# Ordering the large stages of a two-layer encoder trunk from a job list, with 110 seven-product pairs

## The chip, the cores and the metric

The kernel runs on one core of a Trainium2 chip. The time is device microseconds for one execution; the median of three runs of the kernel before is 2484.49 us (2484.1 to 2484.86). Five engines matter: TensorE (PE, matmuls, with its weight loads listed as PEld), VectorE (DVE), ScalarE (ACT), GpSimd (POOL) and the queue of SyncE (SP) that issues nearly all transfers. Each engine works through its own instructions in program order and waits for others by semaphores.

## The reference: what is computed

Two layers on a sequence of 256 tokens with 2048 channels, all in float32. Layer 0 mixes tokens with a gated MLP (gMLP), layer 1 with latent attention (MLA, 16 heads); each is followed by a gated MLP with a causal convolution of width 3 over time.

```python
def gmlp_mixer(x, w_in, ln_g, ln_b, w_s, b_s, w_out):
    z = jax.nn.gelu(x @ w_in)                     # 2048 -> 2 x 6144
    u, v = jnp.split(z, 2, axis=-1)
    v = layer_norm(v, ln_g, ln_b)                 # then mixed over windows of 128 tokens with masked w_s
    ...
    return (u * s.reshape(B, S, GM_HALF)) @ w_out # 6144 -> 2048

def conv_ffn(x, w_up, conv_w, conv_b, w_down):
    h = x @ w_up                                  # 2048 -> 2 x 5504
    h = lax.conv_general_dilated(h, conv_w[:, None, :], ...) + conv_b   # three taps per channel, causal
    a, g = jnp.split(h, 2, axis=-1)
    return (jax.nn.silu(g) * a) @ w_down          # 5504 -> 2048

# each sub-layer: x <- layer_norm(ALPHA * x + sublayer(x)); layer 0: gMLP, FFN; layer 1: MLA, FFN
```

## The kernel before

**Matrix products.** Every float32 operand is split into two float32r parts, a high one (ACT's cast, `hi`, `wh` in the profile) and the remainder (a DVE subtraction, `lo`, `wl`). A product of two operands is three matmuls: high x high, high x low, low x high. Weights come from HBM as one 1 MB tile per *step* (two pieces of 512 KB, 128 x 2048 values, `raw`), and a plain step takes two blocks of 128 input channels (`k`) times 1024 output channels for both halves of the 256 tokens: 8 block products of 128 x 512 columns, 24 matmuls.

**Seven-product pairs.** A step marked `seven` computes the same 2 x 2 x 2 block product in the manner of Strassen and Winograd with seven products, 21 matmuls. For this, sums of the weight blocks are made (DVE, in place in `raw`), split again (`th` by ACT, `tl` by DVE), and sums of the activations too (`xs` once per sub-layer, or `sums1` for each pair of a down product). Its products go to four extra PSUM banks (`up_p`, `dn_p`, ...), which are combined by `gather` at the end of the group. Before, 89 steps are marked.

**Stages in order.** v: 6 groups of 8 steps; u: 6 groups, after each of which the gating (transposes `uT`, products `s`, `gates`); wo: 48 steps in two halves (`Down`); boundary; up: 10 groups of 8 steps, each followed by 16 transposes (`ht`) and the convolution (`taps`); two tail steps; dn: 44 steps in two halves; boundary; MLA; boundary; up and dn again; the last norm. A `boundary` finishes the last steps of a down product (three of them, `LATE`, held back), normalises, transposes the new activations and begins the next product; its order is written out by hand.

**Memory.** One pool of 22 slots of 1 MB each (`BIG`) holds weight tiles in all their forms, the activations (four slots), their sums, and results; a plain step needs 2 slots when it is split, a seven-product step 4, and a tile that is loaded and not yet split 1. Small pools hold intermediate tiles (`mid`, 3 tiles; `t2`, 5), and PSUM has 8 banks.

**What sets the order.** Inside the large stages program order is the order in which Python emits the instructions (`Pinned`, line 74 in all rows of the profile). One step of PE work is one tick: `Feed.next` splits up to two steps ahead and loads up to two more, as far as `room` allows, and `Flow` holds small tasks at ticks counted from the present one (`flow.at(2, "mid", ...)`): the parts of `taps`, of `gather`, `out`, `gates`, `split4`, `sums1`. These distances are fixed numbers in the code. `Ordered` does the same for weight loads on the SP queue; residuals, the norm's rows and the gate's tables are issued with `nc.sync` and have no such place.

**Convolution.** For four tiles of 128 channels x 256 tokens, `taps` writes the three scaled copies with ACT out of PSUM (12 operations), adds them shifted with DVE (two operations of 4 x 255 and 4 x 254 values), then `silu` (ACT) and the gate (DVE).

**Attention scores.** Per head and per half of the queries five matmuls of 256 columns go to one PSUM bank; for the first 128 queries only the first 128 keys are read afterwards.

Of the kernel before, what the change touches and what calls it, by code (L numbers as in the profile page):

```python
# [8 lines left out]
F32 = mybir.dt.float32  # L9
# [96 lines left out]
class Feed:  # L106
# [20 lines left out]
    def _close(self):  # L127
        if self.open is not None:
            s, raw = self.open
            for c in self._pairs(s):  # L130
                self.ve.tensor_tensor(c(s.tl), c(raw), c(s.th.bitcast(F32)), ALU.subtract)
            self.open = None

    def _pairs(self, s):

        if s.by_k:
            return [lambda t: t[:, 1024:2048], lambda t: t[:, 0:1024]]
        four = lambda t: t.rearrange("p (a b c) -> p a b c", a=2, b=2)
        return [lambda t: four(t)[:, :, 1], lambda t: four(t)[:, :, 0]]

    def _split(self, between=lambda: None):
# [4 lines left out]
        s.hi, s.lo = self._tile("wh", F32R), self._tile("wl", F32R)  # L146
# [7 lines left out]
        if s.seven:  # L154
            s.th, s.tl = self._tile("th", F32R), self._tile("tl", F32R)
            b21, x, y, b12 = (raw[:, i * 512 : (i + 1) * 512] for i in range(4))
            b22, b11 = (x, y) if s.by_k else (y, x)
            first, second = self._pairs(s)
# [5 lines left out]
            ac.copy(second(s.th), second(raw))  # L164
            self.open = (s, raw)
        self.split += 1

# [16 lines left out]
    def sums(self, s):  # L184

        t2, t1 = (512, 1024) if s.by_k else (1024, 512)
        return [(s.th[:, o : o + 512], s.tl[:, o : o + 512]) for o in (t1, t2, 1536, 0)]
# [40 lines left out]

def placed(pairs, sevens):
# [15 lines left out]
def trunk(ctx: ExitStack, tc: tile.TileContext, x, xT, gm_in, gm_wout, ffn_up, ffn_dn,  # L245
# [40 lines left out]
    def back(src, n_k, sevens):  # L286
        r = []
        for half in range(2):
            o = half * 1024
            for k in back_order(n_k, half):  # L290
                n = min(2, n_k - k)
                r.append(Step([(j * 1024, 1024, src[k + j][:, o : o + 1024]) for j in range(n)], n * 1024,
                              tuple(range(k, k + n)), True, k in sevens[half]))
        return r
# [25 lines left out]
    feed = Feed(sq, ve, ac, big, steps)  # L320
    Pinned.on = Ordered.on = True
# [75 lines left out]
    def split4(src8, q, n, name):  # L397
# [3 lines left out]
        src = src8[:, 2 * (q % 2) : 2 * (q % 2) + 2]  # L401

        def each(f):
            for w, k in ((2, 2),) if n == 4 else ((n // 2, 2), (n // 2 + 1, 1)):
# [3 lines left out]
        each(lambda x, hi, lo: ac.copy(hi, x))  # L408
        flow.at(1, "mid", lambda: each(lambda x, hi, lo: ve.tensor_tensor(lo, x, hi.bitcast(F32), ALU.subtract)))
        return t  # L410
# [27 lines left out]
    def sums1(kk, name):  # L438

        k0, k1 = kk[:, 0, :], kk[:, 1, :]  # L440
        t = tp.tile([P, 4, P], F32, tag="t2", name=f"{name}t", bufs=T2)
        r = tp.tile([P, 2, 512], F32R, tag="mid", name=name, bufs=MID)
        blocks(k0, k1, [t[:, i, :] for i in range(4)])
        flat = t.rearrange("p i t -> p (i t)")
        flow.at(1, "mid", lambda: ac.copy(r[:, 0], flat))
        flow.at(2, "mid", lambda: ve.tensor_tensor(r[:, 1], flat, r[:, 0].bitcast(F32), ALU.subtract))
        return r
# [7 lines left out]
    class Square:  # L455
# [49 lines left out]
        def gather(self, name):  # L505

            e = slot([P, 4, 512], name)
            u2 = tp.tile([P, 512], F32, tag="t2", name=f"{self.tag}u2", bufs=T2)
            p1, p5, p6, p7 = self.p
            ac.copy(e[:, 0], p1)  # L510
            ve.tensor_tensor(u2, e[:, 0], p6, ALU.add)
            ve.tensor_tensor(e[:, 2], u2, p7, ALU.add)
            ve.tensor_tensor(e[:, 1], u2, p5, ALU.add)
            ve.tensor_tensor(e[:, 3], e[:, 2], p5, ALU.add)
            self.e, self.p = e, None

        def out(self, name, func=None):

            z = self.z = slot([P, 4, 512], name) if self.e is None else self.e

            def add():
                for f in range(2):
# [3 lines left out]
            def copy():  # L526
                for f in range(2):
                    for b in range(2):
# [4 lines left out]
                        elif self.e is None:  # L533
                            ac.copy(o, src)

            if self.e is not None:
                flow.at(0, "first", add)
            flow.at(0, "mid", copy)
            return z
# [17 lines left out]
    def square(tag, order, xs, sums, name, room):  # L557

        sq = Square(tag)
        sevens = [i for i, (_, sv) in enumerate(order) if sv]  # L560
        for i in range(len(order)):
            s = tick(room(i))
            sq.step(s, xs, sums, i == len(order) - 1)
            if sevens and i == sevens[-1]:
                flow.at(1, "first", lambda: sq.gather(name))
            tock()
        return sq

    class Down:

        def __init__(self, n_k, src8, sevens, tag):
            self.n_k, self.src8, self.sevens, self.tag = n_k, src8, sevens, tag
            self.hl, self.sums = {}, {}

        def need(self, k, half):
            q = k // 4
            if q not in self.hl:
                self.hl[q] = split4(self.src8[k // 8], q, min(4, self.n_k - 4 * q), f"{self.tag}a{half}_{q}")

        def need_sums(self, k, half):  # L580
            if k in self.sevens[half] and k not in self.sums:
                self.sums[k] = sums1(self.src8[k // 8][:, k % 8 // 2], f"{self.tag}s{half}_{k}")

        def begin(self):
            flow.at(0, "mid", lambda: self.need(0, 0))
            flow.at(1, "mid", lambda: self.need(4, 0))

        def run(self, ln):
            hl, sums = self.hl, self.sums
            for half in range(2):  # L590
# [4 lines left out]
                late = []  # L595
                for i, k in enumerate(order):
                    for j in order[i : i + 4]:
                        flow.at(0, "mid", lambda j=j: self.need(j, half))
                    for j in order[i : i + 5]:
                        flow.at(0, "mid", lambda j=j: self.need_sums(j, half))  # L600
                    left = n - 1 - i
                    if half == 0:
                        s = tick(BIG - 9 - (2 if left < 7 else 0))
                        if left == 6:
                            ln.residual()
                    else:
                        room = BIG - 5 - (k + 7) // 8 - (2 if left < 6 else 0)
                        s = tick(room, splits=2, loads=2 if left > 1 else 1)
                        if left == 5:
                            ln.prep()  # L610
                    if half == 1 and left < LATE:
                        late.append((s, {k // 4: hl[k // 4]}, left == 0))
                        tock()
                        continue
                    sq.step(s, hl, sums, left == 0)
                    rest = order[i + 1 :]
                    if half == 1 or left >= KEEP:
                        if not any(j // 4 == k // 4 for j in rest):
                            del hl[k // 4]
                    if k in sevens:  # L620
                        del sums[k]
                        if not any(j in sevens for j in rest):
                            flow.at(1, "first", lambda sq=sq, half=half: sq.gather(f"{self.tag}e{half}"))
                            flow.at(2, "mid", lambda sq=sq, half=half: ln.add(2 * half, sq))
                    tock()
                if half == 0:
                    for b in range(2):
                        for f in range(2):
                            flow.at(0, "first", lambda b=b, f=f, sq=sq: ln.join(b, f, sq.acc[b][f]))
                            flow.at(1, "mid", lambda b=b, f=f: ln.stat(b, f))  # L630
            flow.flush()
# [70 lines left out]
    class Norm:  # L702
# [21 lines left out]
        def prep(self):  # L724
            i = self.idx
            self.g = slot([P, D], f"lng{i}")
            nc.sync.dma_start(self.g, ln_rows[2 * i : 2 * i + 1, :].to_broadcast([P, D]))
            self.b = slot([P, D], f"lnb{i}")
            nc.sync.dma_start(self.b, ln_rows[2 * i + 1 : 2 * i + 2, :].to_broadcast([P, D]))
# [74 lines left out]
    def tables():  # L804
        nc.sync.dma_start(wTg, w_sT)
        nc.gpsimd.memset(wTg[64:P, :, 0:64], 0.0)
        nc.sync.dma_start(bsb.rearrange("p g i -> p (g i)"), b_s.to_broadcast([P, 1024]))

    def rows():
# [8 lines left out]
        flow.at(1, "mid", copy)  # L818

    for i, q in enumerate(quads):  # L820
        flow.at(2 + i, "mid", lambda q=q: sums.update(sums_quad(xraw[q], q, f"xs0_{q}")))
    flow.at(4, "mid", tables)
    flow.at(6, "post", rows)

# [3 lines left out]

    for gi in range(6):
        base = BIG - 4 - len(quads) - gi  # L830
# [671 lines left out]
```

## Time and profile before

| what | value |
|---|---|
| median of three runs | 2484.49 us |
| the profiled execution's own time | 2485.57 us |
| its span, first to last instruction | 2483.8 us |
| mean granted TensorE clock | 0.998 |
| PE busy | 2470.1 us (99%) |
| PE weight loads busy | 2068.6 us (83%) |
| DVE busy | 2049.6 us (83%) |
| ACT busy | 1444.2 us (58%) |
| HBM read and written | 482.29 MB and 8.39 MB, 198 GB/s over the span |

Busy time counts each engine's time with at least one instruction in flight. Matmuls overlap in their pipeline, so the duration shown for one is longer than the distance from one start to the next; the distance is what adds up. A group of instructions is written as output<-inputs by tile names with buffer numbers left out, then its shapes and count, the busy time in us and the mean of one in ns, and the idle time of the engine right before, with what ended it. The chain of waits follows the work that ended last backwards; its pieces show start, length, engine and output tile, with a count.

### The profile page before, as it was taken

Reading aid. Unit: us, or ns where it says so; the run is one execution under the profiler, and the core shown is the slowest. Engines: PE = TensorE matmul, PEld = TensorE weight load, DVE = VectorE, ACT = ScalarE, POOL = GpSimd, SP = SyncE. Lnnn points to the kernel's source line nnn. Section 1 sums busy time; section 2 is a strip of 40 time slices with the busy share of each in tenths; the row PEclk is TensorE's granted clock in tenths of the full one; section 3 lists DMA queues with packets and bytes.
Section 4 is the critical chain, followed back from the end, with each engine's and each line's share of the span. In section 5 each row is a group of like instructions: output and inputs, shape, how many; then the busy total and the mean of one; then the engine's idle time right before and its main releaser. Section 6 shows DMA issues by size and latency. Waiting matters only on the chain.

```text
span 2483.8 us, 30045 instructions
## 1 busy us (share of the span) xinstructions
PE 2470.1 (99%) x11666; PEld 2068.6 (83%) x11666; DVE 2049.6 (83%) x2121; ACT 1444.2 (58%) x1673; POOL 1.9 (0%) x11
## 2 busy tenths in 40 slices
PE   9999999999999999999999999999999999999998
PEld 7888888888888888888888888988888888888886
DVE  7899888889797678888899887757768888889796
ACT  6455645555454566666665454555466666667552
POOL 0000000000000000000000000000000000000000
PEclk9999999999999999999999999999999999999999
DMA  7555645555666645555456665435555555556664
GB/s 308 191 193 197 206 167 170 202 171 203 220 214 235 229 166 174 204 186 203 153 198 237 226 237 210 173 136 213 203 174 207 171 187 202 189 196 202 226 205 151
DMA packets 119662, 492.64 MB, mean 198 GB/s; under 512 B 13280, under 2 KB 13664, under 8 KB 104928
## 3 DMA queue, kind: packets, MB, share of 16 engines
q1 hardware_dynamic: 118512, 484.31, 55.6%
q10 hardware_dynamic: 1008, 6.42, 0.6%
q8 instruction: 91, 1.49, 0.2%
q14 instruction: 51, 0.42, 0.0%
HBM read 482.29 MB, written 8.39 MB: 198 GB/s over the span
## 4 chain that ended last, share of the span: by engine, by line
PE 98%; DVE 1%; DMA 0%; ACT 0%; issue 0%; DVEq 0%; ACTq 0%
PE up L74 30%; PE dn L74 16%; PE u L74 9%; PE wo L74 9%; PE v L74 9%; PE up_p L74 4%; PE mo L74 4%; PE upf L74 2%; PE dn_p L74 2%; PE v_p L74 2%; PE ht L74 1%; PE u_p L74 1%; PE wo_p L74 1%; PE mkv L74 1%; PE kn L74 1%; PE qn L74 1%
## 5 line engine op out<-in xcount | busy, mean ns | idle before, releaser
L74 DVE TENSOR_TENSOR wl<-raw,wh 128x2048 fp32r<-128x2048 f32 (+3 forms) x456 | 955.5, 2110 | 216.6 <-ACT wh L74 202.9
L74 ACT CAST wh<-raw 128x2048 fp32r<-128x2048 f32 (+3 forms) x456 | 804.3, 1784 | 187.9 <-DMA raw<-in_ffn_up_dram 54.4
L74 PE MATMUL up<-wh,xhl 128*128 128x512 f32 x2056 | 563.8, 390 | 0.0
L74 PEld LDWEIGHTS up<-wh,xhl 128*128 128x128 f32 x2056 | 384.4, 188 | 78.8
L74 ACT CAST th<-raw 128x1024 fp32r<-128x1024 f32 x178 | 188.5, 1088 | 414.2 <-DVE raw L74 342.1
L74 PE MATMUL up<-wl,xhl 128*128 128x512 f32 x1028 | 319.6, 389 | 0.0
L74 DVE TENSOR_TENSOR raw<-raw 128x512 f32<-128x512 f32 x356 | 246.4, 692 | 12.3
L74 DVE TENSOR_TENSOR tl<-raw,th 128x1024 fp32r<-128x1024 f32 x178 | 214.8, 1222 | 20.7 <-ACT th L74 19.6
L74 PEld LDWEIGHTS up<-wl,xhl 128*128 128x128 f32 x1028 | 192.9, 188 | 40.3
L74 ACT ACTIVATE c<-ht,cst 128x256 f32<-128x256 f32 x320 | 160.0, 591 | 83.2 <-PE ht L74 83.2
L74 PE MATMUL wo<-wh,woa 128*128 128x512 f32 x628 | 173.2, 389 | 0.0
L74 PE MATMUL u<-wh,xhl 128*128 128x512 f32 x600 | 166.1, 391 | 0.0
L74 PE MATMUL dn<-wh,dn0a 128*128 128x512 f32 x576 | 158.3, 389 | 0.0
L74 PE MATMUL dn<-wh,dn1a 128*128 128x512 f32 x576 | 158.0, 389 | 0.0
L74 PE MATMUL v<-wh,xhl 128*128 128x512 f32 x558 | 155.2, 393 | 1.6 <-ACT wh L74 1.6
L74 PEld LDWEIGHTS wo<-wh,woa 128*128 128x128 f32 x628 | 117.7, 188 | 24.3
L74 PEld LDWEIGHTS u<-wh,xhl 128*128 128x128 f32 x600 | 111.9, 188 | 22.7
L74 PEld LDWEIGHTS dn<-wh,dn1a 128*128 128x128 f32 x576 | 108.0, 188 | 22.5
L74 PEld LDWEIGHTS dn<-wh,dn0a 128*128 128x128 f32 x576 | 108.0, 188 | 22.4
L74 PEld LDWEIGHTS v<-wh,xhl 128*128 128x128 f32 x558 | 105.6, 189 | 25.2 <-ACT wh L74 2.8
L74 PE MATMUL wo<-wl,woa 128*128 128x512 f32 x314 | 99.5, 389 | 0.0
L74 PE MATMUL u<-wl,xhl 128*128 128x512 f32 x300 | 93.4, 389 | 0.0
(510 smaller groups left out, 3577.7 us busy)
## 6 DMA issues: line engine op xcount, KB each, us to landing
raw<-in_ffn_up_dram SPq DMA_DIRECT2D x320, 512.0 KB, 4.8
raw<-in_ffn_dn_dram SPq DMA_DIRECT2D x172, 512.0 KB, 4.7
raw<-in_gm_in_dram SPq DMA_DIRECT2D x99, 512.0 KB, 4.9
raw<-in_gm_wout_dram SPq DMA_DIRECT2D x96, 512.0 KB, 4.4
raw<-in_gm_in_dram SPq DMA_DIRECT2D x46, 1024.0 KB, 4.9
raw<-in_ml_out_dram SPq DMA_DIRECT2D x16, 1024.0 KB, 4.8
raw<-in_ml_b_dram SPq DMA_DIRECT2D x14, 1024.0 KB, 4.9
raw<-in_ffn_up_dram SPq DMA_DIRECT2D x12, 1024.0 KB, 6.3
```

What stands on the lines that cost most here:

```text
L74: r = f(*args, **kw)
```

## The change

- `Plan` takes the place of ticks in the v, u, wo, up and dn stages. It keeps a clock for DVE (V), ACT (A), PE (P) and SP loads (S), gives every small piece of work a job with a cost (`adds`, `copies`, `maps`), what it must come after, a due time, and what it takes and gives back of slots, banks and small tiles, and emits the ready job that is due first, idle time counting three times. Before each PE step (`step`) it emits what this step needs; transposes (`turn`) are emitted between steps when the plan's clock says that their inputs are ready, and before the first seven-product step of a group at the latest. `drain` ends a stage before a boundary.
- A seven-product step's weight sums are three operations instead of four (a 1024-wide difference, two 512-wide), in another block order; `gather` has three DVE operations instead of four.
- 110 steps are marked instead of 89: six more in each layer's up groups, three more in wo, three more in each dn.
- `taps`: ACT writes one scaled copy per tile with the bias; DVE adds the two other taps with multiply-adds that read PSUM.
- Residuals, norm rows and the gate's tables are issued in program order on the SP queue.
- Scores of the first 128 queries take only the first 128 keys.

```diff
+        self.len = (4.77 if seven else 5.45) * cols / 2048          # Step
...
-            ve.tensor_tensor(b11, b11, b12, ALU.subtract)
-            ve.tensor_tensor(b12, b22, b12, ALU.subtract)
-            ac.copy(first(s.th), first(raw))
-            ve.tensor_tensor(b22, b22, b11, ALU.add)
-            ve.tensor_tensor(b21, b21, b22, ALU.subtract)
+            ve.tensor_tensor(q(raw, 1), two, last, ALU.subtract)
+            ac.copy(q(s.th, 1), q(raw, 1))
+            ve.tensor_tensor(c2, c2, c1, ALU.add)
+            ve.tensor_tensor(c0, c0, c2, ALU.subtract)
...
+def adds(n, k=1):
+    return k * (0.065 + 0.00106 * n)
+def copies(n, k=1):
+    return k * (0.07 + 0.00086 * n)
+def maps(n, k=1):
+    return k * (0.19 + 0.0009 * n)
...
+class Plan:
+    LAG = {"V": 0.16, "A": 0.33, "P": 0.21, "S": 1.9}
...
+    def _prepare(self, j, load=None):
...
+        hi = new("A", copies(cols), lambda: f.cast(j), after, "hi", need={"big": 2})
+        if not s.seven:
+            new("V", adds(cols), lambda: f.low(j), (hi,), "lo", give={"big": 1})
+            return
+        lo = new("V", adds(cols), lambda: f.low(j), (hi,), "lo")
+        one = new("V", adds(1024), lambda: f.sum1(j), (lo,), "t1")
+        th1 = new("A", copies(1024), lambda: f.high(j, 1), (one,), "h1", need={"big": 2})
+        two = new("V", adds(512, 2), lambda: f.sum2(j), (one,), "t2")
+        th2 = new("A", copies(1024), lambda: f.high(j, 0), (two, th1), "h2")
+        l1 = new("V", adds(1024), lambda: f.rest(j, 1), (th1,), "l1")
+        new("V", adds(1024), lambda: f.rest(j, 0), (th2, l1), "l2", give={"big": 1})
...
+            load = self.job("S", 2.9, f._load, self.loads[-1:], step=j, kind="load", need={"big": 1})
...
+    def run(self, must, until):
...
+                t = self._start(j)
+                idle = max(t - self.now[j.eng], 0.0)
+                key = (self._due(j) + 3.0 * idle, t)
...
+    def turnings(self, force=False):
+        while self.turns:
+            j = self.turns[0]
+            ready = lambda: all(a.end is not None for a in j.after) and self._fits(j)
+            if not force and not (ready() and max([a.end for a in j.after] + [j.ready]) <= self.now["P"] + 0.1):
+                return
...
-GROUP_UP = [placed((), ())] + [placed((2, 3), (4, 6))] * 9
-SEVEN_WO = ((8, 16, 24, 32, 40), (14, 20, 26, 32, 38))
-SEVEN_DN = ((8, 16, 24, 32), (12, 18, 26, 34))
+GROUP_UP = [placed((2, 3), (5, 6)), placed((2, 3), (4, 6)), placed((2, 3, 4), (4, 5, 6)), placed((2, 3), (4, 6)), placed((2, 3, 4), (4, 5, 6)), placed((2, 3), (4, 6)), placed((2, 3, 4), (4, 5, 6)), placed((2, 3), (4, 6)), placed((2, 3, 4), (4, 5, 6)), placed((2, 3), (4, 6))]
+SEVEN_WO = ((8, 14, 20, 26, 30, 34, 40), (40, 34, 28, 22, 16, 12))
+SEVEN_DN = ((8, 14, 18, 22, 26, 32), (34, 28, 22, 16, 12))
...
-                nc.sync.dma_start(t, self.src[b])
+                feed.sq.dma_start(t, self.src[b])
...
-                    ac.activation(c[:, 0, i], src, AF.Identity, bias=cst[:, w + 3 : w + 4], scale=cst[:, w + 2 : w + 3])
-                    ac.activation(c[:, 1, i], src, AF.Copy, scale=cst[:, w + 1 : w + 2])
-                    ac.activation(d[:, i], src, AF.Copy, scale=cst[:, w : w + 1])
...
-                ve.tensor_tensor(y[:, :, 1:S], y[:, :, 1:S], c[:, 1, 0:n, 0 : S - 1], ALU.add)
-                ve.tensor_tensor(y[:, :, 2:S], y[:, :, 2:S], d[:, 0:n, 0 : S - 2], ALU.add)
+            def scale(i):
+                F, src = tiles[i]
+                ac.activation(y[:, i], src, AF.Identity, bias=w(F, 3), scale=w(F, 2))
+            def add(i):
+                F, src = tiles[i]
+                for d in (1, 2):
+                    ve.scalar_tensor_tensor(y[:, i, d:S], src[:, 0 : S - d], w(F, 2 - d), y[:, i, d:S], ALU.mult, ALU.add)
...
-            o = sc[:, b * S : (b + 1) * S]
-            mm(o, q[:, 0, c], k[:, 0], b == 0, False)
+            n = (b + 1) * P
+            o = sc[:, b * S : b * S + n]
+            mm(o, q[:, 0, c], k[:, 0, 0:n], b == 0, False)
```

More of the change, by code (lines that the diff above doesn't have):

```diff
@@ L293, in back @@
                               tuple(range(k, k + n)), True, k in sevens[half]))
+        for i, t in zip(range(-LATE, 0), (1.4,) * (LATE - 1) + (12.0,)):
+            r[i].len = t
         return r
@@ L320, in trunk @@
     feed = Feed(sq, ve, ac, big, steps)
+    plan = Plan(feed)
     Pinned.on = Ordered.on = True
@@ L555, in tock, with square @@
         flow.t += 1
-    def square(tag, order, xs, sums, name, room):
+    def square(tag, order, xs, sums, name, keep):
         sq = Square(tag)
         sevens = [i for i, (_, sv) in enumerate(order) if sv]
+        plan.wide = plan.at(feed.used + (sevens[0] if sevens else 8)) + 1.3
         for i in range(len(order)):
-            s = tick(room(i))
-            sq.step(s, xs, sums, i == len(order) - 1)
+            plan.keep = keep[i]
+            k0 = order[i][0] * 2
+            first = sevens and i == sevens[0]
+            after = (sums[k0][1],) if order[i][1] else ()
+            sq.t = plan.step(lambda s: sq.step(s, xs, {k: r for k, (r, _) in sums.items()}, i == len(order) - 1),
+                             after, FIRST_BANKS if i == 0 else SUM_BANKS if first else (), bool(first))
@@ L594, in run @@
                 n = len(order)
-                late = []
+                late, late_hl = [], set()
+                fresh = True
                 for i, k in enumerate(order):
[L597 to L600, printed above, removed]
+                    plan.keep = 1
                     left = n - 1 - i
[L602 to L608, printed above, removed]
+                    for d, j in enumerate(order[i : i + 4]):
+                        self.need(j, half, plan.at(feed.used + d))
+                    if half == 0 and left == 6:
+                        res = plan.job("S", 6.0, ln.residual, due=plan.at(feed.used), need={"big": 2})
+                    if half == 0 and left < 9:
+                        plan.keep = 3 if left > 6 else 1
+                    if half == 1:
+                        plan.last = end_at + 2
@@ L609, in run @@
                         if left == 5:
-                            ln.prep()
+                            plan.job("S", 6.0, ln.prep, due=plan.at(feed.used), need={"big": 2})
+                        plan.keep = 3 if 5 < left < 8 else 1
                     if half == 1 and left < LATE:
-                        late.append((s, {k // 4: hl[k // 4]}, left == 0))
-                        tock()
+                        late.append((plan.hold(), {k // 4: hl[k // 4][0]}, left == 0))
                         continue
-                    sq.step(s, hl, sums, left == 0)
+                    first = k in sevens and fresh
@@ L616, in run @@
+                    fresh = fresh and not first
+                    after = [hl[k // 4][1]] + ([sums[k][1]] if k in sevens else [])
+                    t = plan.step(lambda s: sq.step(s, {q: h for q, (h, _) in hl.items()},
+                                                    {q: r for q, (r, _) in sums.items()}, left == 0),
+                                  after, FIRST_BANKS if i == 0 else SUM_BANKS if first else (), first)
                     rest = order[i + 1 :]
@@ L985, in ffn, with last_turn @@
         quads = seven_quads(GROUP_UP)
+        plan.begin(4, banks=2, t2=1, late=dict())
         for i, q in enumerate(quads):
-            flow.at(3 + i, "mid", lambda q=q: sums.update(
-                sums_quad(both(xhl[q], f"xb{layer}_{q}"), q, f"xs{layer + 1}_{q}")))
-        flow.at(0, "post", lambda: (after(1, 1, None), turned(1, 0, hb)))
+            sums.update(quad_jobs(q, lambda q=q: both(xhl[q], f"xb{layer}_{q}"), f"xs{layer + 1}_{q}", 8.0 + 6 * i, 1))
+        def last_turn():
+            after(1, 1, None)
+            turned(tl_turn.end, 0, hb)
+        tl_turn = plan.turn(0.6, last_turn, ready=2.0, give={"t2": 1})
         def outputs(g, sq):
-            z = sq.out(f"h{layer}_{g}")
+            z, made = sq.out(f"h{layer}_{g}", sq.t, sq.t + 3)
+            turns = []
             def turn(f):
```

570 lines of the change are left out of this document (439 added, 131 removed).

## The prediction

> **What bounds the kernel now.** I read the page first (busy time, then the chain that ended last), and after it what TensorE (PE) waited for.
>
> ```profile
> span 2483.8 us, 30045 instructions
> PE 2470.1 (99%) x11666; PEld 2068.6 (83%) x11666; DVE 2049.6 (83%) x2121; ACT 1444.2 (58%) x1673; POOL 1.9 (0%) x11
> ...
> PE 98%; DVE 1%; DMA 0%; ACT 0%; issue 0%; DVEq 0%; ACTq 0%
> ```
>
> ```profile
> PE v L74 <- ACT wh L74: 1.6, 1, 1.6
> PE warm L74 <- POOL idle L324: 1.3, 1, 1.3
> ```
>
> PE has no wait after the first 7.4 us. So the span is a start of 7.4 us, an unbroken row of matmuls, and a tail behind the last one. The time can fall by exactly the PE work that goes, and it rises by whatever PE has to wait. The chain of work gives the price of the matmuls, and the timeline their smaller kinds:
>
> ```profile
> 7.40 39.32 PE v L74 x165
> ...
> 66.17 2.72 PE v_p L74 x12
> ...
> 541.15 5.44 PE wo L74 x24
> ...
> 2476.18 3.96 DVE res L74 x6
> ```
>
> ```profile
> 308.88 0.39 PE L74 MATMUL s<-wT,v 128*128 128x128 f32 x2
> 309.10 0.27 PE L74 MATMUL uT<-ident,u 128*128 128x128 f32 x1
> ...
> 876.41 1.91 PE L74 MATMUL ht<-ident,h 128*128 128x128 f32 x16
> 878.08 0.71 PE L74 MATMUL up<-wh,xhl 128*128 128x512 f32 x2
> ...
> 1653.28 0.52 PE L74 MATMUL sc<-kn,qn 128*128 128x256 f32 x3
> 1653.64 0.40 PE L74 MATMUL sc<-krr,qr 128*128 128x256 f32 x2
> ```
>
> A 512-column matmul costs 2.72/12 = 0.2267 us, start to start. A plain step is 24 of them (5.44 us), a seven-product step 21 (4.76). A 256-column score matmul costs (1653.64-1653.28)/3 = 0.120; a 128-column transpose (878.08-876.41)/16 = 0.104; the two passes of a plain f32 128-column product 309.10-308.88 = 0.22.
>
> The second engine is VectorE (DVE). Busy time by stage (PE, PEld, DVE, ACT, POOL behind the length): the v groups, the first boundary, one up group, the two halves of dn0:
>
> ```profile
> 48.40:261.00 212.60, 212.60 (x940) 175.99 (x939) 193.37 (x187) 116.66 (x98) 0.00 (x0) 1.00 0.55 199
> ...
> 797.00:833.00 36.00, 36.00 (x179) 29.97 (x179) 27.45 (x33) 15.40 (x17) 0.00 (x0) 1.00 0.63 230
> ...
> 922.00:966.00 44.00, 44.00 (x206) 36.69 (x204) 37.78 (x35) 29.11 (x40) 0.00 (x0) 1.00 0.54 190
> ...
> 1279.50:1390.00 110.50, 110.50 (x489) 91.45 (x489) 93.54 (x89) 65.87 (x68) 0.00 (x0) 1.00 0.62 220
> 1390.00:1504.00 114.00, 114.00 (x505) 94.22 (x504) 100.13 (x99) 59.99 (x46) 0.00 (x0) 1.00 0.60 215
> ```
>
> DVE stands at 91% in the v groups, and PE still waits for nothing there. The up groups (86%) and dn0 (193.67 of 224.5, 86%) have the room that the change spends.
>
> **The change, part by part.** Costs of DVE and ACT come from the groups of instructions with shapes kept apart (busy time, then the mean of one):
>
> ```profile
> L74 DVE TENSOR_TENSOR wl<-raw,wh 128x2048 fp32r<-128x2048 f32 x334 | 758.4, 2287 | 112.4 <-ACT wh L74 102.5 <-issue 8.6 <-DMA raw<-in_ffn_up_dram 1.1
> L74 DVE TENSOR_TENSOR raw<-raw 128x512 f32<-128x512 f32 x356 | 246.4, 692 | 12.3
> L74 DVE TENSOR_TENSOR tl<-raw,th 128x1024 fp32r<-128x1024 f32 x178 | 214.8, 1222 | 20.7 <-ACT th L74 19.6 <-PE wo L74 1.0
> L74 DVE TENSOR_TENSOR wl<-raw,wh 128x1536 fp32r<-128x1536 f32 x89 | 156.1, 1754 | 99.6 <-ACT wh L74 95.9 <-PE u L74 1.7 <-PE u_p L74 1.4
> L74 DVE TENSOR_TENSOR c<-c,d 128x1016 f32<-128x1016 f32 x42 | 51.1, 1217 | 1.4
> L74 DVE TENSOR_TENSOR c<-c 128x1020 f32<-128x1020 f32 x42 | 51.0, 1215 | 0.0
> L74 DVE SCALAR_TENSOR_TENSOR sg<-s,cst,sb 128x256 f32<-128x256 f32 x48 | 20.9, 478 | 23.7 <-PE s L74 23.7
> L74 DVE TENSOR_TENSOR dn0a<-act,dn0a 128x1024 fp32r<-128x1024 f32 x19 | 23.2, 1219 | 1.2 <-ACT dn0a L74 1.2
> ```
>
> 1. *More seven-product pairs.* 178 casts' remainders, two per pair, are 89 pairs before; the new lists hold 15 (v) + 12 (u) + 48 (up) + 13 (wo) + 22 (dn) = 110. 21 more pairs drop 3 matmuls each: 63 x 0.2267 = **-14.3 us**, all of it on the path.
>
> 2. *Narrower scores.* In each of 16 heads five matmuls shrink from 256 to 128 columns: 80 in all. No row shows this kind of matmul with 128 columns. From 512 to 256 columns the price falls by 0.107; going on like that it would be 0.067 (-4.3 us). If it fell back to the two-pass product it would be 0.22 (+8.0). I take the transposes' 0.104, the nearest row with 128 columns: 80 x 0.016 = **-1.3 us**.
>
> The Trainium skill ("VectorE: DVE Perf Modes", the errata section's table) prices a matmul at max(60, 6 + columns) cycles of 2.4 GHz, an estimate of 0.056 us at 128 columns; the sum would then be 3.9 us lower still. At 256 it gives 0.109, where the trace has 0.120.
>
> 3. *What a pair costs DVE.* Before: 1.75 + 4 x 0.69 + 2 x 1.21 = 6.93 us against 758.4/334 = 2.27 for a plain step. The rewrite makes one 1024-wide difference of two 512-wide ones, so 1.75 + 1.22 + 2 x 0.69 + 2.41 = 6.77. Each new pair adds 4.5 us, each old one gives back 0.17. In the down products a pair also needs its activation sums (four 128-wide operations and one 512-wide remainder):
>
> ```profile
> 1324.89 0.29 DVE L74 SCALAR_TENSOR_TENSOR dn0s_24t<-act 128x128 f32<-128x128 f32 x1
> ...
> 1325.82 4.49 DVE L74 TENSOR_TENSOR wl<-raw,wh 128x2048 fp32r<-128x2048 f32 x2
> 1330.22 0.68 DVE L74 TENSOR_TENSOR dn0s<-dn0s_24t,dn0s 128x512 fp32r<-128x512 f32 x1
> ```
>
> that is 0.93 + 0.68 = 1.6 us, so 8.4 us of DVE beside 4.76 us of PE.
>
> 4. *Taps by VectorE.* Of 12 ACT operations per four tiles 8 go, which frees ACT (58% busy, no bound). DVE does eight 255-wide multiply-adds out of PSUM in place of two long adds. The gate's operation has the same form: 20.9/48 = 0.44 us. 8 x 0.44 = 3.5 against 1.2 + 1.2 = 2.4: +1.1 us per four tiles, +2.2 per up group.
>
> The Trainium skill speaks against this ("VectorE: DVE Perf Modes", rules for kernel authors): copy a matmul's output to SBUF first if many operations follow, and keep the operation count low. By its (120 + 255) cycles of 0.96 GHz, an estimate, a tap would be 0.39 us and the group 0.8 us cheaper than by the row.
>
> 5. *The sums, stage by stage.* An up group with two pairs: 37.8 - 0.5 (merged adds, pairs and gather) + 2.2 = 39.5 us of DVE in 43.9 of PE, 90%. One with three pairs: 37.8 - 0.7 + 4.5 + 2.2 = 43.8 in 43.2: **0.6 us too much**. There are four of these per layer, each behind one with 4.4 us to spare. In dn the first half now runs k = 14 to 26 as pair, plain, pair, plain, pair, plain, pair: PE 4 x 4.76 + 3 x 5.44 = 35.4; DVE 4 x 8.4 + 3 x 2.27 + 3.5 activation remainders of 1.22 = 44.7. That is 9.3 too much, behind seven steps (one pair) with 37.4 - 26.3 = 11.1 to spare. In wo k = 26 to 34 has three pairs in five steps: 25.2 against 32.8, 7.6 too much. All these hold only if earlier slack can be spent in advance, and the 22 slots limit that: with four for the activations, two for their sums and up to six for results, about 10 to 13 remain, which is the running step and two more. I take 0.4 us of stall per three-pair group (two thirds of the excess, 8 x 0.4 = 3.2) and 1 us for each of the three dense runs: **+6 us**. The bounds are 0 (all carried) and 8 x 0.6 + 2 x 9.3 + 7.6 = 31 (nothing carried).
>
> 6. *The order itself.* Program order now comes from the job list, with its own costs: a 255-wide tap counts 0.065 + 0.00106 x 255 = 0.335, not 0.44. Per up group DVE is 16 x 0.105 = 1.7 us behind the plan. What PE has queued behind a late DVE sum: the transposes of the group's result stand at a point where the plan holds them ready, and all later matmuls wait behind them. The cover is DVE's lead, one plain step's 2.27 us or more; I take nothing, at most 20 x 1.7 = 34 us. Residuals, norm rows and the gate's tables are issued on the SP queue in written order now, ahead of weight loads that could pass before; such a pair of tiles is 2 MB. The cover is two steps of loads (10 us); without it, the plan's own 2 x 2.9 = 5.8 us per place. The four boundaries keep their code (DVE 27.45 of 36): nothing.
>
> Sum for the profiled execution: 2483.8 - 14.3 - 1.3 + 6 = 2474.2 us of span. That execution took 2485.57 and the median is 2484.49, 0.7 above the span, so **2475 us**.
>
> **The rivals.**
>
> *All is carried* (0 stall): 2484.5 - 14.3 - 1.3 = 2469; for it speaks the v stage, 91% without a wait; against it the excess of point 5. With the cheap score price 2466.
>
> *DVE becomes the bound in the dense runs.* Place: the pairs at k = 14 to 26 of both dn and 26 to 34 of wo. If the lead is one step and not three, most of 9.3 + 9.3 + 7.6 is paid, with the up groups' 4.8: 31 us, so 2484.5 - 15.6 + 31 = 2500, **slower**. It decides once the stalls exceed 20 us. For it: 44.7 against 35.4, and the slots. Against it: 11 us of slack directly ahead.
>
> *The plan is too optimistic* (point 6): PE waits at its transposes half of the 1.7 us in each of 20 groups, 17 us: 2484.5 - 15.6 + 17 = 2486, no change. Against it: sparse groups have 4.4 us to catch up.
>
> *Scores fall back to two passes*: 2484.5 - 14.3 + 8 + 6 = 2484, no change. For it only that no narrow matmul of that kind is in the trace.
>
> **How the numbers follow.** Changes under 0.2% (5 us) can't be told from none. Forecast 0.50 and all-carried 0.16 make faster 0.66; plan too optimistic 0.12 and scores 0.07 make no change 0.19; dense runs bound, slower, 0.15. The range goes from 2466 (all carried, cheap scores) to 2490, where the stalls reach 21 us, two thirds of the upper bound, and the slower cases begin; the forecast's own range is 2469 to 2480.
>
> **What would show it.** PE matmuls of 512 columns fall by 63 and keep 0.2267 us (granted clock 1.00); if PE's list of waits stays short, all is carried. The forecast has waits on DVE (wl, tl, xs or h) of some 6 us, in three-pair groups and dense runs. Waits in transposes mean point 6; long waits around dn k = 14 to 26 mean the slower rival. Start-to-start of the five narrow scores tells point 2, the taps' mean (0.44) point 4, and DVE's share in the up groups (about 95%) point 5. The prediction is wrong if stalls exceed 10 us or an item that I took at nothing shows as a wait.

## The result, and the profile after

The kernel after takes **2469.71 us** (median of four runs, 2469.09 to 2470.75) against 2484.40 beside it: 14.7 us less, ratio 0.9941 [0.9928, 0.9953]. The forecast was 2475; the value that came is that of the rival *all is carried*, 2469.

The page of the kernel after, span and busy time, then the chain of work by engine:

```profile
span 2467.7 us, 30002 instructions
...
PE 2454.2 (99%) x11603; PEld 2054.8 (83%) x11603; DVE 2195.8 (89%) x2429; ACT 1367.6 (55%) x1376; POOL 1.9 (0%) x11
...
PE 95%; DVE 4%; issue 1%; DMA 0%; ACT 0%; DVEq 0%; SPq 0%; ACTq 0%
```

PE runs 11603 matmuls, exactly 63 fewer. DVE has 146 us more to do and stands at 89% of a shorter span; ACT has 77 us less. DVE now takes 4% of the chain instead of 1%: in places PE runs on the last sum that DVE has just finished.

PE's complete list of waits in the kernel after:

```profile
PE v L75 <- ACT wh L75: 1.4, 1, 1.4
PE warm L75 <- POOL idle L646: 1.3, 1, 1.3
PE up L75 <- DVE h L75: 0.2, 1, 0.2
```

Two waits belong to the start, as before. Of the 6 us that the forecast expected behind DVE, 0.2 came.

Busy time by stretch of the kernel after (length; PE, PEld, DVE, ACT and POOL busy with counts; granted clock, DMA share, GB/s): the u stage, an up group with two pairs, the next one with three, and the dense run of the first half of dn:

```profile
259.65:539.47 279.82, 279.82 (x1357) 235.59 (x1357) 233.14 (x243) 158.82 (x164) 0.00 (x0) 1.00 0.53 181
...
960.70:1004.60 43.90, 43.90 (x203) 36.58 (x202) 41.20 (x45) 24.89 (x25) 0.00 (x0) 1.00 0.60 208
1004.60:1047.90 43.30, 43.30 (x200) 36.09 (x200) 42.02 (x48) 23.69 (x25) 0.00 (x0) 1.00 0.46 158
1303.00:1338.00 35.00, 35.00 (x156) 28.97 (x156) 34.62 (x41) 20.70 (x19) 0.00 (x0) 1.00 0.60 205
```

The two groups hold 41.20 + 42.02 = 83.2 us of DVE work, and the forecast's two sums, 39.5 + 43.8, make 83.3. Only the split differs: by these sums, 1.7 us that belong to the three-pair group are done in the sparse one ahead of it. The three other such pairs of groups in this layer hold 83.9, 83.0 and 81.3 us. In dn's dense run (DVE works on it somewhat ahead of PE, which takes its steps from 1309 to 1345 us) DVE is busy 34.62 of 35.00 us while PE has no gap. The prediction counts 44.7 us of DVE work for that run, so it lives on work done before it.

The spans differ by more (2483.8 - 2467.7 = 16.1) than the medians, mainly because the profiled execution of before was itself 1.1 above its median. Its granted clock was low at the start:

```profile
7.00:9.00 2.00, 1.93 (x7) 1.30 (x6) 1.09 (x3) 1.74 (x3) 0.00 (x0) 0.73 1.04 421
9.00:10.50 1.50, 1.50 (x5) 1.19 (x4) 1.50 (x3) 1.20 (x2) 0.00 (x0) 0.50 1.07 432
10.50:12.00 1.50, 1.50 (x6) 1.19 (x5) 1.50 (x2) 1.42 (x2) 0.00 (x0) 0.72 1.01 429
```

In the execution of after the same three stretches have 1.00. At the granted shares above, 2.00 x 0.27 + 1.50 x 0.50 + 1.50 x 0.28 = 1.7 us of clock was lost in that one execution of before. The medians are the fair comparison.

### The profile page after: what moved, and what is told of

Read it like the earlier page. It is cut to its first block, busy times and chain, and to the rows that moved or that the text cites. A ratio compares the mean times of both kernels' runs of the same rounds, so it can differ in the third digit from the quotient of the medians.

```text
span 2467.7 us, 30002 instructions
## 1 busy us (share of the span) xinstructions
PE 2454.2 (99%) x11603; PEld 2054.8 (83%) x11603; DVE 2195.8 (89%) x2429; ACT 1367.6 (55%) x1376; POOL 1.9 (0%) x11
## 4 chain that ended last, share of the span: by engine, by line
PE 95%; DVE 4%; issue 1%; DMA 0%; ACT 0%; DVEq 0%; SPq 0%; ACTq 0%
PE up L75 28%; PE dn L75 13%; PE u L75 9%; PE wo L75 9%; PE v L75 9%; PE up_p L75 5%; PE mo L75 4%; PE dn_p L75 2%; PE upf L75 2%; PE v_p L75 2%; PE wo_p L75 1%; PE ht L75 1%; PE u_p L75 1%; DVE wl L75 1%; PE mkv L75 1%; PE kn L75 1%
## 5 line engine op out<-in xcount | busy, mean ns | idle before, releaser
L75 PE MATMUL up<-wh,xhl 128*128 128x512 f32 x1888 | 522.1, 390 | 0.2 <-DVE h L75 0.2
L75 ACT CAST th<-raw 128x1024 fp32r<-128x1024 f32 x220 | 230.9, 1053 | 330.7 <-DVE raw L75 327.7
L75 PEld LDWEIGHTS up<-wh,xhl 128*128 128x128 f32 x1888 | 352.9, 188 | 72.8 <-issue 0.6
L75 PE MATMUL up<-wl,xhl 128*128 128x512 f32 x944 | 294.7, 389 | 0.0
L75 DVE TENSOR_TENSOR raw<-raw 128x1024 f32<-128x1024 f32 x330 | 286.4, 868 | 8.8
L75 DVE TENSOR_TENSOR tl<-raw,th 128x1024 fp32r<-128x1024 f32 x220 | 265.4, 1219 | 7.9 <-ACT th L75 6.5
L75 PEld LDWEIGHTS up<-wl,xhl 128*128 128x128 f32 x944 | 177.1, 188 | 37.0 <-DVE wl L75 0.2
L75 DVE SCALAR_TENSOR_TENSOR y<-ht,cst,y 128x255 f32<-128x255 f32 x320 | 147.4, 479 | 14.1 <-ACT y L75 8.4
L75 PEld LDWEIGHTS dn<-wh,dn1a 128*128 128x128 f32 x534 | 100.2, 188 | 20.8
L75 ACT ACTIVATE y<-ht,cst 128x256 f32<-128x256 f32 x160 | 77.3, 574 | 64.4 <-PE ht L75 62.3
L75 PE MATMUL up_p<-th,xs 128*128 128x512 f32 x288 | 96.4, 389 | 0.0
```

The source lines that it names most:

```text
L75: r = f(*args, **kw)
```

## The experiments

Each experiment is compared with the median of after, 2469.71. The kernel before, measured again beside the experiments, had medians of 2484.40 to 2484.86, so differences under 0.5 us mean nothing.

**The order without the pairs** (order_only). The kernel after with the three lists of before (89 pairs); job list, DVE taps and narrow scores stay.

```diff
-GROUP_UP = [placed((2, 3), (5, 6)), placed((2, 3), (4, 6)), placed((2, 3, 4), (4, 5, 6)), ...]
-SEVEN_WO = ((8, 14, 20, 26, 30, 34, 40), (40, 34, 28, 22, 16, 12))
-SEVEN_DN = ((8, 14, 18, 22, 26, 32), (34, 28, 22, 16, 12))
+GROUP_UP = [placed((), ())] + [placed((2, 3), (4, 6))] * 9
+SEVEN_WO = ((8, 16, 24, 32, 40), (14, 20, 26, 32, 38))
+SEVEN_DN = ((8, 16, 24, 32), (12, 18, 26, 34))
```

> The changed kernel with the 89 seven-product pairs of the kernel before: job list, taps by VectorE and narrow scores stay. If the gain is the dropped matmuls alone, 63 x 0.2267 = 14.3 us come back: 2469.7 + 14.3 = 2484.0 (2483 to 2485). If the new order saves time by itself, it stays at 2480 or less; if the order costs something that the pairs hide, 2486 or more.

Measured 2483.86 (2482.73 to 2484.3), ratio 0.9998 [0.9988, 1.0007]. The order by itself, with the taps by DVE and the narrow scores, gains nothing that can be told from none, and 2483.86 - 2469.71 = 14.15 us are the 21 pairs, priced at 14.3.

**The pairs without the order** (pairs_only). The kernel before, with its ticks and ACT's taps, and the new lists.

```diff
-GROUP_UP = [placed((), ())] + [placed((2, 3), (4, 6))] * 9
-SEVEN_WO = ((8, 16, 24, 32, 40), (14, 20, 26, 32, 38))
-SEVEN_DN = ((8, 16, 24, 32), (12, 18, 26, 34))
+GROUP_UP = [placed((2, 3), (5, 6)), placed((2, 3), (4, 6)), placed((2, 3, 4), (4, 5, 6)), ...]
+SEVEN_WO = ((8, 14, 20, 26, 30, 34, 40), (40, 34, 28, 22, 16, 12))
+SEVEN_DN = ((8, 14, 18, 22, 26, 32), (34, 28, 22, 16, 12))
```

> The kernel before, ticks and taps by ScalarE as they were, with the 110 pairs. If the order is not needed, 2484.4 - 14.3 = 2470.1 (within 1). If the fixed ticks can't keep VectorE ahead in three-pair groups and dense runs, PE waits for wl, tl or the activation sums, and the time lies between 2473 and 2490.

Measured **2534.66** (2533.49 to 2535.54), ratio 1.0203 [1.0188, 1.0218]: 50 us slower than before, 65 us slower than after with the same pairs, and outside both expectations. PE's largest waits in it:

```profile
PE up L74 <- DVE wl L74: 18.6, 19, 3.2
PE up_p L74 <- DVE tl L74: 11.8, 15, 1.0
PE dn L74 <- DVE wl L74: 7.7, 6, 1.3
PE up_p L74 <- ACT th L74: 4.7, 10, 0.5
```

Windows of pairs_only (columns as above): from the transposes of one up group to the next with two pairs in between, and then with three:

```profile
969.10:1013.00 43.90, 43.90 (x203) 36.59 (x202) 38.70 (x36) 29.04 (x39) 0.00 (x0) 1.00 0.58 198
1013.00:1061.00 48.00, 45.11 (x204) 36.13 (x203) 41.65 (x40) 30.62 (x41) 0.00 (x0) 1.00 0.43 153
```

In the sparse group DVE idles 5.2 of 43.9 us, where the kernel after has 41.20 busy; the dense one then takes 48 us instead of 43.3, and PE stands 2.9 of them. Stage by stage and against after, pairs_only loses 26.5 and 27 us in the two layers' up groups and 5.5 and 4.6 in dn, and nothing in wo, though wo has three more pairs too. The chain of waits of pairs_only in that dense group (start, length, what):

```profile
1013.17 0.45 PE ht L74 x4
...
1013.64 0.89 ACT c L74 x2
...
1024.61 0.94 ACT th L74
...
1047.73 2.29 DVE wl L74
...
1050.06 5.05 PE up L74 x21
```

It begins with the transposes. From 1013.64 to 1024.61 ACT works on 24 scaled copies, with the cast `wh` of the first pair in their middle (1018.30) and `th` behind them. DVE's timeline shows what that costs (in brackets the wait):

```profile
1019.89 1.76 DVE L74 TENSOR_TENSOR wl<-raw,wh 128x1536 fp32r<-128x1536 f32 x1 [4.81 <-ACT wh L74]
...
1025.57 2.36 DVE L74 TENSOR_TENSOR tl<-raw,th 128x1024 fp32r<-128x1024 f32 x2 [1.02 <-ACT th L74]
```

DVE stands 4.81 us for `wh` and 1.02 for `th`, and does not catch up until 1050. So ACT counts here too, although it is busy only 58% of the span: what matters is the place of these casts among the copies. This run changes order and taps together; the next two kernels take the taps apart.

**ACT's taps in the new order** (act_taps). ACT writes three scaled copies and DVE adds with two long operations, as jobs of the plan; the copies need one of the large slots.

```diff
-            y = tp.tile([P, 4, S], F32, tag="mid", name=f"y{name}", bufs=MID)
+            c = slot([P, 2, 4, S], f"c{name}")
+            d = tp.tile([P, 4, S], F32, tag="mid", name=f"d{name}", bufs=MID)
...
-                    ve.scalar_tensor_tensor(y[:, i, d:S], src[:, 0 : S - d], w(F, 2 - d), y[:, i, d:S], ALU.mult, ALU.add)
...
+                ac.activation(c[:, 1, i], src, AF.Copy, scale=cst[:, w + 1 : w + 2])
+                ac.activation(d[:, i], src, AF.Copy, scale=cst[:, w : w + 1])
...
+                ve.tensor_tensor(u[:, :, 1:S], u[:, :, 1:S], c[:, 1, 0:n, 0 : S - 1], ALU.add)
+                ve.tensor_tensor(u[:, :, 2:S], u[:, :, 2:S], d[:, 0:n, 0 : S - 2], ALU.add)
```

> The changed kernel with the taps as before (three scaled copies by ScalarE into one slot of the large pool and one small tile, two long adds by VectorE), all as jobs of the plan. VectorE loses about 40 us of work (42 x 1.1), ScalarE gains about 170. If PE is fed either way, 2469.7 within 1. If the taps by VectorE are what makes room (the slot that the copies take, or ScalarE's time), PE waits and it is 2472 to 2485.

Measured 2480.43 (2477.57 to 2482.29), ratio 0.9984 [0.9974, 0.9993]: 10.7 us slower than after, although DVE's busy time falls from 2195.8 to 2152.6. Its page and its largest wait of PE:

```profile
PE 2456.5 (99%) x11603; PEld 2054.9 (83%) x11603; DVE 2152.6 (87%) x2173; ACT 1491.0 (60%) x1720; POOL 1.9 (0%) x11
```

```profile
PE up_p L75 <- DVE tl L75: 5.0, 4, 1.8
```

So 43 us less DVE work did not help, and DVE's total alone does not decide. It also shows what the order (with the merged weight sums and the narrow scores) is worth while the pairs and ACT's taps are held: 2534.66 - 2480.43 = 54 us of the 65. How these 54 divide between the order, the merged sums and the rest was not measured.

**DVE's taps with a large slot** (taps_slot). The taps as in after, their result in one of the 22 slots instead of a small tile.

```diff
-            y = tp.tile([P, 4, S], F32, tag="mid", name=f"y{name}", bufs=MID)
+            y = slot([P, 4, S], f"y{name}")
...
-                             need={} if i else {"mid": 1})
+                             need={} if i else {"big": 1})
...
```

> The changed kernel, taps by VectorE, but the tap's result lies in a slot of the large pool from the first copy to the gate, as it did when ScalarE made three copies; no work is added or taken. If the slot is what made the kernel with taps by ScalarE wait (10.7 us over the changed kernel), this one lands near it, 2476 to 2484. If ScalarE's added 170 us or the later release of PSUM did it, 2469.7 within 1.5.

Measured 2473.07 (2471.06 to 2473.29), ratio 0.9951 [0.9936, 0.9966], 3.4 us above after and between the two expectations. One slot for this time costs about a third of what ACT's taps cost; the trace, of the fastest of the four executions (2471.06), has only 0.4 us of PE's waits behind DVE and does not say where. The other 7 us, ACT's 123 us more or its later release of PSUM, were not separated.

**Two slots fewer** (less_slots2). The plan alone sees 20 slots.

```diff
-        self.room = dict(big=[0.0] * (BIG - held - n), ...)
+        self.room = dict(big=[0.0] * (BIG - 2 - held - n), ...)
```

> The changed kernel with two of the 22 slots hidden from the plan in all its stages (the pool itself stays). If VectorE's lead, which the slots bound, carries the three-pair groups and the dense runs, PE waits there: 2475 to 2500, with waits for wl and tl in up and dn. If the due times alone do it and lead has reserve, 2469.7 within 1.5.

Measured 2487.76 (2486.68 to 2488.53), ratio 1.0011 [1.0002, 1.0021]: 18.0 us above after, the whole 14.7 us of the change and 3 us more. PE's largest waits in it:

```profile
PE dn L75 <- DVE wl L75: 6.8, 2, 3.4
PE up_p L75 <- DVE tl L75: 1.7, 2, 0.9
PE up L75 <- DVE wl L75: 1.6, 2, 0.8
```

By stage dn pays 6.5 and 4.7, up 2.0 and 2.4 in the two layers. The two long waits, 3.4 us each, stand at the very start of dn (they end at 1279.13 and 2246.36) and not in its dense run. DVE's timeline ahead of the first:

```profile
1269.52 7.36 DVE L75 SCALAR_TENSOR_TENSOR y<-ht,cst,y 128x255 f32<-128x255 f32 x16 [1.01 <-ACT y L75]
1276.79 4.48 DVE L75 TENSOR_TENSOR wl<-raw,wh 128x2048 fp32r<-128x2048 f32 x2
```

The 16 taps of the last up group form a block of 7.36 us in DVE's queue, and the remainder that dn needs lies behind it. In after the same block costs nothing: from the last pair of up to this block DVE has made five remainders there, and three here. The work is the same; what went is how far DVE may run ahead, and the slots bound that. Whether 20 slots would carry dn's dense run, this kernel does not tell, since DVE gained on PE during the wait just ahead of it.

**More DVE work without slots** (gate_twice). The 42 gate operations of 0.69 us are issued twice, into the same tile, about 29 us more.

```diff
-                ve.tensor_tensor(act[a // 8][:, a % 8 // 2, 0:m, :], s[:, 0:m], y[:, 0:m], ALU.mult)
+                for _ in range(2):
+                    ve.tensor_tensor(act[a // 8][:, a % 8 // 2, 0:m, :], s[:, 0:m], y[:, 0:m], ALU.mult)
```

> The changed kernel with the gate's product of the two up stages written twice (the same values to the same place): 42 more VectorE operations of about 0.65 us, 27 us in all, no slot, no bank and no ScalarE work more; the plan knows the doubled cost. VectorE comes to 83.2 + 2.7 = 85.9 of 87.2 us in two up groups, 98.5%. If slots alone set the lead, 2469.7 within 1. If VectorE's time is the limit too, as with three pairs in every group, it is 2471 to 2476.

Measured 2478.25 (2477.3 to 2478.79), ratio 0.9974 [0.9964, 0.9984], 8.5 above after and above the expected range. A group with two pairs in it:

```profile
960.70:1004.60 43.90, 43.90 (x204) 36.57 (x203) 43.08 (x48) 24.96 (x26) 0.00 (x0) 1.00 0.55 188
```

DVE has 0.8 us left in a group that had 2.7, and PE still has no gap in it. PE's waits come later:

```profile
PE dn L75 <- DVE wl L75: 3.5, 4, 1.0
PE up_p L75 <- DVE tl L75: 2.2, 2, 1.1
```

The two behind `tl` stand in the last three-pair group of each layer. Of the four behind `wl` the three long ones, 1.0 us each, stand in dn's dense runs (1338, 2290 and 2301 us), where no work was added: DVE comes there with less lead. About 30% of the added work reaches the end, so DVE time is a limit beside the slots, with little of it to spare. (The doubled operation also holds its small tiles some 0.7 us longer.)

**Three pairs in all up groups but the first** (up_three). 120 pairs.

```diff
+GROUP_UP = [placed((2, 3), (5, 6))] + [placed((2, 3, 4), (4, 5, 6))] * 9
```

> The changed kernel with three pairs in all up groups but the first (five more per layer, 120 pairs). PE loses 30 x 0.2267 = 6.8 us: 2462.9 if all is carried. VectorE has 83.2 us in two groups now; with one more pair 87.7 in 86.4, 1.3 us too much per two groups and no sparse group to hide it: 2 x 4.5 x 1.3 = 12 us of waits, 2475. If lead alone counted and not the mean load, it would stay under 2466.

Measured 2483.77 (2482.59 to 2485.38), ratio 0.9997 [0.9988, 1.0007]: ten more pairs take 6.8 us of matmuls away and the time rises by 14.1. A group of it:

```profile
960.00:1004.00 44.00, 43.83 (x201) 35.92 (x200) 43.48 (x49) 25.09 (x27) 0.00 (x0) 1.00 0.55 192
```

Here DVE is the bound: 43.48 of 44.00, in a period that PE alone would do in 43.2. Without a sparse group in between there is nothing to carry from, and PE's four long waits (7.8 us behind `tl`) come late in each up stage, at 1122 and 1206 us in the first layer, when the lead is used up. The direction was expected; the size, 8.8 above the 2475, was not.

**Three pairs in a row in the u groups** (u_three). 116 pairs (110 and six more); DVE had 46.7 us to spare in the u stage (279.82 - 233.14).

```diff
-GROUP_U = [placed((2, 3), (4, 6))] * 6
+GROUP_U = [placed((2, 3, 4), (4, 5, 6))] * 6
```

> The changed kernel with three pairs in each of the six u groups (112 + 4 = 116 pairs). PE loses 18 x 0.2267 = 4.1 us: 2465.6 if it is fed. VectorE goes from 233 us to 233 + 6 x 4.5 = 260 in 276 of that stage (94%), below the share of the up groups now (95%), so I expect 2465 to 2467. If the v results, which hold six slots there, leave too little lead, 2469 or more with waits in u_p.

Measured 2490.52 (2487.45 to 2492.86), ratio 1.0023 [1.0013, 1.0032]: 20.8 above after in place of 4.1 below. The expectation counted DVE's time alone and failed. The chain of waits in the first group:

```profile
288.43 0.69 PE u_p L75 x3
289.12 0.12 SPq L75
...
289.29 6.13 DMA raw<-in_gm_in_dram
...
295.52 1.91 ACT wh L75
...
297.45 2.30 DVE wl L75
...
299.80 12.18 PE u L75 x46
```

Three pairs in a row hold 12 slots. The plain step behind them gets its slot only when PE has finished, at 289.12, with a tile of the second of the three; then load, cast and remainder run one after another until 299.80, 10.7 us later. The slots, and not DVE, set this time.

The windows of u_three around it (columns as above):

```profile
294.00:297.00 3.00, 2.75 (x13) 1.94 (x11) 0.00 (x0) 1.48 (x1) 0.00 (x0) 1.00 1.00 335
297.00:300.00 3.00, 0.93 (x3) 0.50 (x4) 2.29 (x1) 1.02 (x2) 0.00 (x0) 0.92 1.00 292
300.00:303.00 3.00, 3.00 (x8) 2.33 (x9) 1.68 (x1) 2.84 (x3) 0.00 (x0) 0.51 1.01 399
303.00:306.00 3.00, 3.00 (x15) 2.46 (x14) 2.93 (x4) 2.03 (x5) 0.00 (x0) 1.00 0.56 167
```

From 294 to 297 DVE has nothing to do. PE is idle 0.25 + 2.07 us in six, and in the next three the granted clock is 0.51: 8 matmuls start where 15 do in the three after. The gap is paid once as idle time and again as slow matmuls.

**The same pairs, spaced** (u_three_spaced). Steps 2, 4 and 6 of each u group.

```diff
-GROUP_U = [placed((2, 3), (4, 6))] * 6
+GROUP_U = [placed((2, 3, 4), (2, 4, 6))] * 6
```

> Three pairs in every u group again (116 pairs), now at steps 2, 4 and 6 with a plain step between two of them, as the v groups have them, and not at 4, 5 and 6. If the slots that three pairs in a row hold made the u groups wait, they are fed now: 2469.7 - 4.1 = 2465.6 (up to 2467). If VectorE's load of 94% there or the six slots of the v results are the limit in any order, it stays above 2470.

Measured 2471.5 (2470.85 to 2472.3), ratio 0.9947 [0.9932, 0.9962]: 19 us better than in a row, with the same matmuls and the same DVE work. So the place of the pairs is shown as the cause of these 19 us. It is still 1.8 above after instead of 4.1 below, above 2470, so by the expectation's second sentence some limit remains in this order too. Its u stage:

```profile
259.20:540.90 281.70, 278.81 (x1338) 231.31 (x1337) 254.88 (x271) 166.87 (x175) 0.00 (x0) 1.00 0.53 180
```

The stage takes 281.7 us where 279.8 - 4.1 = 275.7 was to be had. 2.9 us of it is PE standing, near all of it in the last group, behind the gate's operations and a remainder. By the last section's reckoning the five waits there are each some 0.16 longer than listed, 0.8 us in all; where the other 2 went stays open.

**Spaced, in every second u group** (u_alternate_spaced). 113 pairs.

```diff
-GROUP_U = [placed((2, 3), (4, 6))] * 6
+GROUP_U = [placed((2, 3, 4), (2, 4, 6)), placed((2, 3), (4, 6))] * 3
```

> Three spaced pairs in every second u group, two in the others (113 pairs): 9 matmuls fewer than the changed kernel, 2469.7 - 2.0 = 2467.7 if fed. If three pairs need a sparse group ahead of them, this one is the faster of the two spaced ones; if not, it lies 2 us above the other.

Measured 2469.07 (2468.13 to 2469.63), ratio 0.9937 [0.9922, 0.9951], 0.6 below after: not to be told from it, and 1.4 above what the dropped matmuls promise. It is 2.4 faster than the version with three pairs in every group, as it should be if three pairs need a sparse group ahead of them. No version that clearly beats the kernel after was found.

**A truer price for the taps** (tap_cost). The plan counts 0.94 us for a tile's two taps instead of 0.67.

```diff
-                made.append(plan.job("V", adds(255, 2), ...
+                made.append(plan.job("V", 0.94, ...
```

> The changed kernel whose plan counts a tile's two tap operations at 0.94 us, as the trace has them, in place of 0.67. Work, slots and pairs are the same; only the order moves. If the plan's too low cost made PE wait anywhere, this would show it: up to 1 us less. By the trace, where PE waits 0.2 us in all, 2469.7 within 0.7.

Measured 2471.31 (2470.16 to 2471.85), ratio 0.9945 [0.9931, 0.996], 1.6 above after and outside its expectation, with one new wait of 1.0 us in a boundary. The better price gives no better order.

**Wide scores** (wide_scores). All score products on 256 columns again.

```diff
-            n = (b + 1) * P
+            n = 2 * P
```

> The changed kernel with 256 columns in all score matmuls again, as before the change. The two traces show a head's ten score matmuls at 1.19 us before and 1.15 after, so 16 x 0.04 = 0.6 us: 2470.3. By the prediction's 0.016 us per matmul it would be 1.3: 2471.0; by the price of the wider kinds carried on (0.053 each) 4.2: 2473.9.

Measured 2470.29 (2469.43 to 2470.82), ratio 0.9944 [0.9929, 0.9959], 0.58 above after: of the size that the trace gives, but within what the runs differ.

## Why the prediction was right, and where it was off

*Point 1* holds: 63 matmuls fewer, 14.3 us predicted, 14.15 between order_only and after.

*Point 2* was too large by half. The timeline of one head in the kernel after (start, length of the piece, what, count):

```profile
1643.44 0.45 PE L75 MATMUL sc<-kn,qn 128*128 128x128 f32 x3
1643.73 0.39 PE L75 MATMUL sc<-krr,qr 128*128 128x128 f32 x2
1643.95 0.57 PE L75 MATMUL sc<-kn,qn 128*128 128x256 f32 x3
1644.36 0.40 PE L75 MATMUL sc<-krr,qr 128*128 128x256 f32 x2
1644.59 0.63 PE L75 MATMUL mo<-wh,oT 128*128 128x512 f32 x2
```

Five narrow matmuls take 1643.95 - 1643.44 = 0.51 us, 0.102 each, near the transposes' 0.104. But the five wide ones behind them now take 0.64, 0.128 each against 0.120 before. A head saves 0.04, sixteen 0.6 us instead of 1.3. The estimate of 0.056 us from the errata table of the Trainium skill ("VectorE: DVE Perf Modes") is not borne out for this kind of matmul, which takes 0.102.

*Points 3 and 4.* The groups of DVE with shapes kept apart, kernel after:

```profile
L75 DVE TENSOR_TENSOR raw<-raw 128x512 f32<-128x512 f32 x220 | 152.0, 691 | 6.4
L75 DVE TENSOR_TENSOR raw<-raw 128x1024 f32<-128x1024 f32 x110 | 134.4, 1222 | 2.3
L75 DVE SCALAR_TENSOR_TENSOR y<-ht,cst,y 128x254 f32<-128x254 f32 x160 | 77.1, 482 | 5.7
L75 DVE SCALAR_TENSOR_TENSOR y<-ht,cst,y 128x255 f32<-128x255 f32 x160 | 76.1, 476 | 8.4 <-ACT y L75 8.4
```

The sums of the weights cost what the rows of before gave. A tap costs 0.48 us (77.1/160) and not 0.44. The gate's row gave both: 20.9/48 is busy time, in which gate operations overlap a little, and its mean of one is 478 ns; the taps don't overlap, so the mean was the number to take. The estimate of 0.39 us from the errata table of the Trainium skill ("VectorE: DVE Perf Modes") was further off. The rule of the Trainium skill ("VectorE: DVE Perf Modes", Rules for kernel authors) is to accept reading PSUM or to copy it out first if many operations follow. Only two follow for each tile here, and the copies by ACT did save DVE 43 us, but the kernel with them took 2480.43 against 2469.71; one slot's use is part of that.

*Point 5* is the term that was mis-sized: **6 us of stall, measured 0.2**. Less the 0.7 us of point 2, it accounts for most of the 5.3 us between the 2475 of the forecast and the 2469.71 that came, which lies at the low end of the forecast's own range. The sums of DVE's work were right to 0.1 us for the two up groups shown, in part by luck: the other pairs of groups differ from the sum by up to 2 us, and the 32 taps at 0.04 us too little would alone make 1.3. What was wrong is the share that slack can carry. I took two thirds of a group's excess as lost; the plan moves 1.7 us of the dense group's work into the sparse group, so that the two stand at 94% and 97% (41.20 of 43.90, 42.02 of 43.30) and neither is over. The dense runs, taken at 1 us each, cost nothing either. The idea behind the step stands, though: two slots fewer cost 18.0 us and 29 us more of DVE work 8.5, so lead is what carries, with little to spare. But with fewer slots the largest loss came at the start of dn, which the prediction did not name. The margin was mis-sized, not the mechanism.

*Point 6* holds in the form in which it was put: with 89 pairs the order, with the taps and the scores, is worth 0.5 us, which is nothing. But it left out what pairs_only shows: it priced the order only by what it could cost, and never asked whether the ticks could use DVE's slack for 110 pairs. With ticks the same pairs make the kernel 50 us slower than before. The tap price was indeed below the real one, and mending it changes nothing for the better.

Of the rivals, *all is carried* came true (given 0.16). *DVE becomes the bound in the dense runs* is false for 110 pairs in this order; with 120 (up_three) DVE becomes the bound, but in the up groups. *The plan is too optimistic* and *scores fall back* are out: no wait at a transpose, no two-pass price.

## What to carry to other kernels

An engine's share of busy time does not tell whether more work fits: what counts is the slack that lies directly ahead of a dense stretch and the buffers in which work done early can be kept; to measure that lead, take a buffer or two away (here 2 of 22 slots, 18 us), add work that needs none (29 us, 8.5 us), and look where the waits then stand, since it need not be the dense stretch. Put the steps that hold most buffers apart from each other, since the step behind them starts its load when they let go (19 us between 4, 5, 6 and 2, 4, 6). A reordering that gives nothing alone can be what makes another change pay, so try both parts alone before either is dropped.

## What the runs showed of the hardware that was not expected

Short gaps can lower the clock. In u_three gaps of 0.72 and 1.59 us between matmuls, 2.3 us in six, were followed by about 3 us at a granted clock of 0.51 (the windows above). Its next four u groups repeat this: 3.3 us at 0.50 from 350.8, 402.0, 453.2 and 504.4 us. The Trainium skill ("TensorE: Matmul & The Clock Gate", Why this matters for your kernels) says to avoid idle gaps over about 3 us; no single gap here was that long. One gap of 1.84 us was enough in up_three, twice (0.50 in the 3.4 us from 1206.6 and 2172.6), but one of 2.03 us in the same kernel was not (1.00 from 1122.0), nor one of 1.79 us in act_taps (1.00 from 1121.0). So length alone does not decide; what does was not found. Smaller gaps left it alone: in the dense group of pairs_only PE stands 2.89 us in 48, in pieces, at a clock of 1.00. In less_slots2 the clock is 0.50 for 3.3 to 3.4 us behind each of the two long waits, so some 1.7 us more is lost each time.

PE's waits understate the loss. In pairs_only all of PE's listed waits in up and dn make 42.8 us, but its span is 64.0 us longer than that of after; PE's busy time is 21.3 us longer too, with the same 11603 matmuls:

```profile
PE 2475.5 (98%) x11603; PEld 2054.9 (81%) x11603; DVE 2174.8 (86%) x2320; ACT 1478.9 (58%) x1720; POOL 1.9 (0%) x11
```

One part shows in its timeline (in brackets the wait):

```profile
1041.10 0.39 PE L74 MATMUL up<-wh,xhl 128*128 128x512 f32 x1
1041.94 0.50 PE L74 MATMUL up<-wl,xhl 128*128 128x512 f32 x1 [0.46 <-DVE wl L74]
```

From start to start it is 0.84 us where 0.2267 is the rule, 0.61 lost, and the wait is given as 0.46: a matmul's shown duration of 0.39 reaches over the first 0.16 of each gap. The four lists hold 50 waits, so this makes about 50 x 0.16 = 8 us. The lower granted clock (0.996 against 0.999 over the span) is another part: behind two waits of 3.2 us it is 0.51, 0.50 and 0.50 in stretches (857.6 to 861.0, 861.0 to 864.5, 1850.9 to 1854.3 us) in which PE is busy 2.19, 3.50 and 3.01 us, so about half of these, 4 us, is lost. The other 9 of the 21.3 us are not explained.
